# Tile 0's layer norm among tile 1's first products, and low parts issued at once at the joints and in the opening

## The chip, the cores and the metric

The kernel runs on one core of one Trainium2 chip. The metric is the device time of one execution in microseconds. Of the kernel before there are three timed runs, with a median of 1212.61 us (1208.63 to 1213.71), and one profiled execution.

## The reference

A decoder trunk in float32: 256 tokens, model width 1024, two layers. Each layer is a half-step FFN, a mixer and a second half-step FFN, each between two RMS norms (before: `pre`, after: `post`):

```python
for l in range(DEPTH):
    h = rms_norm(x, ffn1_pre_g[l])
    x = x + 0.5 * rms_norm(swiglu(h, ffn1_w1[l], ffn1_w2[l]), ffn1_post_g[l])
    h = rms_norm(x, mix_pre_g[l])
    q, k, v, u_s, v_s, g_a, g_b = jnp.split(h @ w_in[l], IN_SPLIT_POINTS, axis=-1)
    y_attn = sliding_window_attention(q, k, v, attn_sinks[l])
    y_sgu = spatial_gating(gelu(u_s), gelu(v_s), sgu_ln_g[l], sgu_ln_b[l], sgu_w[l], sgu_b[l])
    merged = sigmoid(g_a) * (y_attn @ w_attn_branch[l]) + sigmoid(g_b) * (y_sgu @ w_sgu_branch[l])
    x = x + rms_norm(merged @ w_out[l], mix_post_g[l])
    h = rms_norm(x, ffn2_pre_g[l])
    x = x + 0.5 * rms_norm(swiglu(h, ffn2_w1[l], ffn2_w2[l]), ffn2_post_g[l])
```

FFNs are 2816 wide (SwiGLU). Attention has 16 query heads and 2 key/value heads of 64, a window of 128 and one sink logit for each head. `spatial_gating` takes a layer norm of gelu(v_s) and mixes it over the tokens of a chunk of 128 with a lower triangular matrix. The two branches meet in the merge.

## The kernel before

**Split products.** Every float32 product is done in three passes of TensorE on a reduced format: an operand is split into a high part (its rounding) and a low part (what is left), and high x high, high x low and low x high are summed in a bank (`passes`, L249; `feature_major`, L256 to L258; `feature_pair`, L269). The 256 tokens are two tiles of 128, tile 0 and tile 1.

**Weights.** All weights come as *units*, slices of 128x1024 in the order of use. SP loads a unit into one of four `raw` buffers; ScalarE makes its high part (`wh`, L137), VectorE its low part (`wl`, the subtraction L149). Both go into a ring of nine pairs, or, for the first four units of a sub-layer, into buffers of other tensors (named `m` or `n`). The low part is the last reader of a raw buffer: the load of unit u+4 is issued behind it and waits for it. `Stream.upto(n)` splits all units below n. The low part lags one unit: `upto` issues the cast of unit u, then the low part of unit u-1, and u stays *pending* (`self.rest`) until the next unit is split or a product asks for it:

```python
                self.ready += 1
                self.low()
                self.rest = u
```

**Order.** It is a manual schedule: each engine executes its instructions in the order in which the code emits them. So where a step stands in the code decides what stands behind it in its engine's queue.

**The opening.** The normalisation of the first FFN's input and its first eight units are written out by hand (from L958 on): transposes, the weighing with the gain (`weigh`, L934), splits, products in parts. It ends with `subs[0].prepare()` and `finish`.

**A sub-layer** begins with *first products* (`FirstFFN`: eight units; `FirstMix`: ten, units 0 to 7 for v_s and 8 and 9 for v and k), which have the tokens as rows. `middle` does the rest with features as rows: in an FFN the columns of SwiGLU (first pass L269, sums L624 and L625, Silu L627); in a mixer, pair by pair, u (units 10 to 17), q (units 18 to 25), the gates and the two branches. Attention steps are put into slots of that sequence (`ATTEND`); scores start with L710, which takes q from `evac_q`: ScalarE writes the scaled high part (L834), VectorE the low part (L837).

**A joint** is where one sub-layer's last products and the next one's first meet. There are five: two into mixers, three into FFNs. `project` writes it: a loop over the second matrix's units but the last four; `head(t)`, which finishes tile t's sum with those four (ScalarE squares it, L174; VectorE weighs the result with the post gain, L434); the reciprocal root of the total (`total`, L204; `rsqrt`, L182 to L197); the sum onto x and its weighing with the next gain (L438, L443); transposes (L214, copied by L517, low part L521); the first products of tile 0, of which some steps already run ahead of tile 1's; then tile 1's. Near tile 0's products `st.upto(fence)` splits the next sub-layer's first units, the last of them pending.

In tile 1's loop there is one more step:

```python
            if i == 10:
                turn0()
            s()
            if i % 2:
                st.upto(min(st.ready + 1, first.units[-1] + 1 + AHEAD))
```

`rest` has 12 steps. In a mixer these are four for units 4 to 7 (six products each), then eight for units 8 and 9 (three each); ahead of the loop stand 24 products (`hi + lo`). `turn0` is tile 0's second half of `finish`. In an FFN it transposes the hidden values and splits them. In a mixer it transposes the keys (L375), ScalarE takes their high part (`kth`, L376), VectorE their low part (`ktl`, L379), and then VectorE does tile 0's layer norm of v_s (from L384 on; its last operations are two of 128x1024). Tile 1's (`turn1`) runs during the u products.

Of the kernel before, what the change touches and what calls it, by code (L numbers as in the profile page):

```python
# [63 lines left out]
def trunk(ctx: ExitStack, tc: tile.TileContext, a: dict, out: bass.AP):  # L64
# [24 lines left out]
    def new(p, shape, tag, dt=F32, **kw):  # L89
        ids[0] += 1  # L90
        return p.tile(shape, dt, tag=tag, name=f"{tag}_{ids[0]}", **kw)
# [8 lines left out]
    class Stream:  # L100
        def __init__(self):
            self.src, self.where = [], []
            self.raw, self.split = {}, {}
            self.loaded = self.ready = 0
            self.free = RING
            self.rest = None

        def add(self, src, where="ring"):
            self.src.append(src)
            self.where.append(where)  # L110
            return len(self.src) - 1
# [9 lines left out]
        def upto(self, n, spare=0):  # L121


            while self.ready < min(n, len(self.src)):
                u = self.ready
                if self.where[u] == "ring":
                    if self.free <= spare:
                        return
                    self.free -= 1
                self.load(u + 1)  # L130
                if self.where[u] == "ring":
                    h, lo = new(ring, [P, 1024], "wh", F32R), new(ring, [P, 1024], "wl", F32R)
                else:
                    at = self.where[u]
                    both = new({"m8": m8, "n8": n8}[at], [P, 2, 1024], at, F32R)
                    h, lo = both[:, 0, :], both[:, 1, :]
                nc.scalar.copy(h, self.raw[u])  # L137
                self.split[u] = (h, lo)
                self.ready += 1
                self.low()  # L140
                self.rest = u

        def low(self):

            if self.rest is not None:
                u = self.rest
                self.rest = None
                h, lo = self.split[u]
                nc.vector.tensor_tensor(out=lo, in0=self.raw.pop(u), in1=f(h), op=ALU.subtract)  # L149
                self.load(u + 1 + RAW)  # L150
# [11 lines left out]
    st = Stream()  # L162
# [6 lines left out]
    def halves():  # L169
        return [slice(h * 512, (h + 1) * 512) for h in range(2)]  # L170
# [61 lines left out]
    def spread(dg):  # L232

        n = dg.shape[1]
        ps = bank()[:, 0:n * P]
        nc.tensor.matmul(ps, ones, flat(dg), start=True, stop=True)
        rb = new(t2, [P, n, P], "t2")
        nc.scalar.copy(flat(rb), ps)
        return rb

    def bc4(ap):
        return ap.unsqueeze(1).to_broadcast([P, 4, P])
# [30 lines left out]
    class FirstFFN:  # L273
# [23 lines left out]
            return hi, lo, rest, one  # L297

        late = 11

        def finish(self, t, r, hts):

            o = self.o[t]
            s = new(t2, [P, 512], "t2")
            hh = new(t2, [P, 512], "t2")
            if r is None:
                nc.scalar.activation(s, o[0], AF.Silu)
                nc.vector.tensor_tensor(out=hh, in0=s, in1=o[1], op=ALU.mult)
            else:
                nc.scalar.activation(s, o[0], AF.Silu, scale=r)  # L310
                nc.vector.scalar_tensor_tensor(out=hh, in0=o[1], scalar=r, in1=s, op0=ALU.mult, op1=ALU.mult)

            def turn():
                split(hts[0][0][:, 0:FA, rows_of(t)], hts[0][1][:, 0:FA, rows_of(t)], transpose4(hh, 0))
            return turn

    class FirstMix:
# [33 lines left out]
            return hi, lo, rest  # L351

        late = 6

        def finish(self, t, r, kv):
            vs, vv, kth, ktl, lng, lnb = kv
# [41 lines left out]
    def project(units, lhs, k_post, gpost, gpre, nxt, xt, behind=None):  # L398
# [7 lines left out]
        def one(t, c, h, b):  # L406
            lh, ll = lhs(c)
            wh, wl = st[units[c]]
            passes(o[t][h], lh[:, rows_of(t)], ll[:, rows_of(t)], wh[:, b], wl[:, b], (0, 1, 2), c == 0, c == n - 1)
# [4 lines left out]
        for c in range(n0):  # L414
            if behind:
                behind(c, 0)
            for t in range(NT):
                for h, b in enumerate(halves()):
                    one(t, c, h, b)
            st.done(units[c])  # L420
            if behind:
                behind(c, 1)
            left = n0 - 1 - c
            st.upto(min(end + lead[left], fence) if left < len(lead) else min(units[c] + AHEAD + 1, end))

        parts = [new(tiny2, [P, 2], "parts") for _ in range(NT)]
        og = [new(t4, [P, D], "t4") for _ in range(NT)]
# [17 lines left out]
        def scale(t, r):  # L445
            for b in halves():
                nc.vector.tensor_scalar(out=og[t][:, b], in0=og[t][:, b], scalar1=r, scalar2=None, op0=ALU.mult)
# [60 lines left out]
        first = nxt.first  # L508

        def turn(t, h):  # L510
            return transpose4(og[t], h * 4)

        def quarter(t, h):
            return og[t].rearrange("p (a b) -> p a b", a=KD)[:, h * 4:h * 4 + 4, :]

        def high(t, h, ps):
            nc.scalar.copy(xth[:, h * 4:h * 4 + 4, rows_of(t)], ps)  # L517

        def low(t, h, ps):
            at = (slice(None), slice(h * 4, h * 4 + 4), rows_of(t))  # L520
            nc.vector.tensor_tensor(out=xtl[at], in0=ps, in1=f(xth[at]), op=ALU.subtract)  # L521
# [40 lines left out]
        dg = diagonal([r0])  # L562
        scale(1, rn)
        st.upto(fence)
        for i, s in enumerate(rest):
            if i == first.late:
                turned = [turn(1, h) for h in range(2)]
                for h in range(2):
                    high(1, h, turned[h])
                    low(1, h, turned[h])  # L570
                rb = spread(dg)
                for h in range(2):
                    nc.vector.tensor_tensor(out=quarter(0, h), in0=ps[h], in1=bc4(rb[:, 0, :]), op=ALU.mult)
            s()
        nxt.prepare()
        turn0 = first.finish(0, r0, nxt.into)
# [5 lines left out]
        for i, s in enumerate(rest):  # L582
            if i == 0:
                for h in range(2):
                    high(0, h, quarter(0, h))
                    low(0, h, quarter(0, h))
            if i == 10:
                turn0()
            s()
            if i % 2:  # L590
                st.upto(min(st.ready + 1, first.units[-1] + 1 + AHEAD))
        return first.finish(1, None, nxt.into)

    class FFN:
# [16 lines left out]
        def middle(self, xt, xth, xtl, turn1, early):  # L611
            for _ in range(2):
                self.into.append((new(m8, [P, 8, S], "m8", F32R), new(m8, [P, 8, S], "m8", F32R)))
            for c in range(FA, FC):
                o = [bank(), bank()]
                us = self.cols[(c - FA) * 2:(c - FA) * 2 + 2]
                for half in range(2):
                    feature_pair(o[half], us[half], xt)
                if c == FA + 2:
                    turn1()  # L620
                s = new(t2, [P, 512], "t2")
                y = s.rearrange("p (a b) -> p a b", a=2)
                for half in range(2):
                    nc.scalar.copy(y[:, half, :], o[half][:, S:2 * S])  # L624
                    nc.vector.tensor_tensor(out=y[:, half, :], in0=o[half][:, 0:S], in1=y[:, half, :], op=ALU.add)  # L625
                    if half == 0:
                        nc.scalar.activation(y[:, 0, :], y[:, 0, :], AF.Silu)  # L627
                nc.vector.tensor_tensor(out=y[:, 1, :], in0=y[:, 0, :], in1=y[:, 1, :], op=ALU.mult)
                st.upto(us[1] + 1 + AHEAD)
                hh, hl = self.lhs(c)  # L630
                split(hh, hl, s[:, S:2 * S])
                if c == FA + 2:
                    early()
# [291 lines left out]
    first = subs[0].first  # L925
# [95 lines left out]
    subs[0].prepare()  # L1021
    turns = [first.finish(t, r01[t], subs[0].into) for t in range(NT)]

    def turn1():
        for turn in turns:
            turn()

    for i, sub in enumerate(subs):
        last = i == len(subs) - 1
        nxt = None if last else subs[i + 1]  # L1030
        gains = []

        def early():

            gains.append(gain(sub.post, i // 3))
            if not last:
                gains.append(gain(nxt.pre, (i + 1) // 3))
            if i == 0:
                nc.sync.dma_start(sinks, a["attn_sinks"].unsqueeze(0).partition_broadcast(P))
            if isinstance(nxt, Mix):  # L1040
                nxt.tables()

        behind = sub.middle(both, *xt, turn1, early)
        turn1 = project(sub.rows, sub.lhs, sub.k_post, gains[0], None if last else gains[1], nxt, xt, behind)
# [54 lines left out]
```

## Time and profile before

| | |
|---|---|
| time, median of 3 runs | 1212.61 us (1208.63 to 1213.71) |
| the profiled execution | 1208.95 us, its span 1207.0 us |
| mean granted TensorE clock | 0.993 |
| TensorE matmul busy (PE) | 1179.5 us, 98% |
| TensorE weight load busy (PEld, beside PE) | 1048.6 us, 87% |
| VectorE busy (DVE) | 836.0 us, 69% |
| ScalarE busy (ACT) | 678.4 us, 56% |
| GpSimd busy (POOL) | 60.0 us, 5% |
| moved by DMA | 220.89 MB, mean 183 GB/s |

The span runs from the first to the last recorded instruction; the time of the execution is 1.95 us longer. Busy shares are means over stages that differ: VectorE, at 69%, is full in a joint and has room in between. Of VectorE's 836.0 us, 454.6 are the 372 low parts of weights (L149, 1250 ns each), and of ScalarE's 678.4 the 372 casts take 382.9 (1049 ns each).

### The profile page before, as it was taken

Reading aid. Unit: us, or ns where it says so; the run is one execution under the profiler, and the core shown is the slowest. Engines: PE = TensorE matmul, PEld = TensorE weight load, DVE = VectorE, ACT = ScalarE, POOL = GpSimd, SP = SyncE. Lnnn points to the kernel's source line nnn. Section 1 sums busy time; section 2 is a strip of 40 time slices with the busy share of each in tenths; the row PEclk is TensorE's granted clock in tenths of the full one; section 3 lists DMA queues with packets and bytes.
Section 4 is the critical chain, followed back from the end, with each engine's and each line's share of the span. In section 5 each row is a group of like instructions: output and inputs, shape, how many; then the busy total and the mean of one; then the engine's idle time right before and its main releaser. Section 6 shows DMA issues by size and latency. Waiting matters only on the chain.

```text
span 1207.0 us, 18394 instructions
## 1 busy us (share of the span) xinstructions
PE 1179.5 (98%) x7031; PEld 1048.6 (87%) x7031; DVE 836.0 (69%) x1423; ACT 678.4 (56%) x1143; POOL 60.0 (5%) x40
## 2 busy tenths in 40 slices
PE   8999999999999999999999999999899999999997
PEld 6788888899999888888888888879899997888886
DVE  6768747678775877676576766576868768676653
ACT  5656634457676555655445655454567664665541
POOL 0000000000212200000000000000012030000000
PEclk9999999999999999999999999999999999999999
DMA  6577673465446636658636657735544664555660
GB/s 227 190 244 228 232 237 115 138 241 157 123 145 201 196 105 228 208 178 261 206 102 221 218 181 257 228 102 175 181 152 122 187 194 128 177 206 184 198 211 35
DMA packets 61287, 220.89 MB, mean 183 GB/s; under 512 B 7056, under 2 KB 7056, under 8 KB 61200
## 3 DMA queue, kind: packets, MB, share of 16 engines
q1 hardware_dynamic: 60912, 219.46, 56.0%
q8 instruction: 55, 0.90, 0.3%
q10 hardware_dynamic: 288, 0.27, 0.1%
q14 instruction: 32, 0.26, 0.1%
HBM read 218.65 MB, written 1.05 MB: 182 GB/s over the span
## 4 chain that ended last, share of the span: by engine, by line
PE 83%; DVE 10%; DMA 3%; ACT 2%; issue 1%; SPq 0%; DVEq 0%; ACTq 0%
PE mm L269 32%; PE mm L249 31%; PE mm L256 5%; PE mm L257 5%; PE mm L258 5%; DMA raw<-in_w_in 2%; DVE wl L149 2%; DMA raw<-in_ffn_w 1%; PE mm L747 1%; DVE x L438 1%; DVE rt L193 1%; PE mm L214 1%; ACT wh L137 1%; DVE t L443 1%; PE mm L710 1%
## 5 line engine op out<-in xcount | busy, mean ns | idle before, releaser
L149 DVE TENSOR_TENSOR wl<-raw,wh 128x1024 fp32r<-128x1024 f32 x372 | 454.6, 1250 | 112.8 <-ACT wh L137 111.8
L137 ACT CAST wh<-raw 128x1024 fp32r<-128x1024 f32 x372 | 382.9, 1049 | 183.0 <-DMA raw<-in_ffn_w 76.6
L269 PE MATMUL mm<-xt,wh 128*128 128x512 f32 x1152 | 290.7, 393 | 1.1 <-ACT t L310 0.9
L249 PE MATMUL mm<-wh,m 128*128 128x512 f32 x832 | 258.8, 390 | 0.0
L269 PEld LDWEIGHTS mm<-xt,wh 128*128 128x128 f32 x1152 | 207.6, 189 | 38.5 <-ACT t L310 1.2
L249 PEld LDWEIGHTS mm<-wh,m 128*128 128x128 f32 x832 | 156.3, 188 | 32.1
L269 PEld LDWEIGHTS mm<-xt,wl 128*128 128x128 f32 x1152 | 157.1, 191 | 11.8 <-DVE wl L149 0.6
L249 PE MATMUL mm<-wl,m 128*128 128x512 f32 x416 | 162.1, 390 | 0.0
L269 PE MATMUL mm<-xt,wl 128*128 128x256 f32 x1152 | 160.8, 283 | 0.2 <-DVE wl L149 0.2
L256 PE MATMUL mm<-xt,wh 128*128 128x256 f32 x512 | 147.7, 288 | 0.0
L258 PE MATMUL mm<-xt,wl 128*128 128x256 f32 x512 | 146.2, 286 | 0.0
L257 PE MATMUL mm<-xt,wh 128*128 128x256 f32 x512 | 146.2, 286 | 0.0
L625 DVE TENSOR_TENSOR t<-mm,t 128x256 f32<-128x256 f32 x144 | 60.7, 422 | 97.4 <-ACT t L624 97.4
L256 PEld LDWEIGHTS mm<-xt,wh 128*128 128x128 f32 x512 | 99.7, 195 | 0.2
L257 PEld LDWEIGHTS mm<-xt,wh 128*128 128x128 f32 x512 | 99.6, 195 | 0.2
L258 PEld LDWEIGHTS mm<-xt,wl 128*128 128x128 f32 x512 | 99.5, 194 | 0.0
L249 PEld LDWEIGHTS mm<-wl,m 128*128 128x128 f32 x416 | 78.2, 188 | 15.8
L624 ACT COPY t<-mm 128x256 f32<-128x256 f32 x144 | 52.9, 368 | 46.6 <-PE mm L269 46.3
L256 PE MATMUL mm<-m,wh 128*128 128x256 f32 x256 | 72.7, 284 | 0.0
L258 PE MATMUL mm<-m,wl 128*128 128x256 f32 x256 | 72.5, 283 | 0.0
L257 PE MATMUL mm<-m,wh 128*128 128x256 f32 x256 | 72.5, 283 | 0.0
L627 ACT ACTIVATE t<-t 128x256 f32<-128x256 f32 x72 | 30.1, 418 | 74.8 <-DVE t L625 74.8
(156 smaller groups left out, 1331.4 us busy)
## 6 DMA issues: line engine op xcount, KB each, us to landing
raw<-in_ffn_w SPq DMA_DIRECT2D x264, 512.0 KB, 4.4
raw<-in_w_in SPq DMA_DIRECT2D x84, 512.0 KB, 4.3
raw<-in_w_sgu_branch SPq DMA_DIRECT2D x16, 512.0 KB, 3.6
raw<-in_w_attn_branch SPq DMA_DIRECT2D x16, 512.0 KB, 4.3
raw<-in_w_out SPq DMA_DIRECT2D x16, 512.0 KB, 4.6
gain<-in_ffn_post_g SPq DMA_DIRECT2D x4, 512.0 KB, 5.8
gain<-in_ffn_pre_g SPq DMA_DIRECT2D x3, 512.0 KB, 7.5
x<-in_x SPq DMA_DIRECT2D x4, 256.0 KB, 4.4
```

The lines of the kernel that those rows point to most:

```text
L137: nc.scalar.copy(h, self.raw[u])
L149: nc.vector.tensor_tensor(out=lo, in0=self.raw.pop(u), in1=f(h), op=ALU.subtract)
L193: nc.vector.scalar_tensor_tensor(out=t, in0=y, scalar=w, in1=y, op0=ALU.mult, op1=ALU.mult)
L214: nc.tensor.transpose(ps[:, k, :], src[:, (c0 + k) * P:(c0 + k + 1) * P], ident)
L249: nc.tensor.matmul(o, every[i][0], every[i][1], start=start and i == 0, stop=stop and i == 2)
L256: nc.tensor.matmul(o, wh[:, ks], ah[:, k, :], start=(k == 0), stop=False)
L257: nc.tensor.matmul(o, wh[:, ks], al[:, k, :], start=False, stop=False)
L258: nc.tensor.matmul(o, wl[:, ks], ah[:, k, :], start=False, stop=(k == KD - 1))
L269: nc.tensor.matmul(out_, w[:, k * P:(k + 1) * P], x, start=(i == 0), stop=(i == len(todo) - 1))
L624: nc.scalar.copy(y[:, half, :], o[half][:, S:2 * S])
L625: nc.vector.tensor_tensor(out=y[:, half, :], in0=o[half][:, 0:S], in1=y[:, half, :], op=ALU.add)
L627: nc.scalar.activation(y[:, 0, :], y[:, 0, :], AF.Silu)
```

## The change

Three things are edited.

1. A flag `slip` in `Stream`. While it is false, `upto` issues the low part of a unit right behind its own cast, so that none is pending. It is false in the opening and becomes true behind the first FFN's `finish`.
2. In `project`, `st.low()` behind the loop and again behind `st.upto(fence)`: the pending unit's low part is issued at once. The first place is ahead of `head(0)` and so of L434; the second is ahead of tile 0's remaining first products.
3. `turn0` goes into tile 1's loop at a step that the first products name: 10 for an FFN, as before, and 2 for a mixer.

```diff
@@ class Stream
             self.rest = None
+            self.slip = False
...
                 self.ready += 1
                 self.low()
                 self.rest = u
+                if not self.slip:
+                    self.low()
@@ class FirstFFN
         late = 11
+        turn0 = 10
@@ class FirstMix
         late = 6
+        turn0 = 2
@@ project
             left = n0 - 1 - c
             st.upto(min(end + lead[left], fence) if left < len(lead) else min(units[c] + AHEAD + 1, end))
+        st.low()
...
         scale(1, rn)
         st.upto(fence)
+        st.low()
         for i, s in enumerate(rest):
...
-            if i == 10:
+            if i == first.turn0:
                 turn0()
@@ opening
     turns = [first.finish(t, r01[t], subs[0].into) for t in range(NT)]
 
+    st.slip = True
+
```

In the rows of the programs' order below, a row is line, operation, result<-operands and shape; names carry a serial number, and line numbers of the changed kernel are a few higher. In VectorE's queue at layer 0's joint into the mixer, `wl_1817` is the low part of unit 7, `wl_1823` that of unit 8, `t_347` (before) and `t_348` (now) the weighed sum. Before:

```order
L149 TENSOR_TENSOR wl_1793<-raw_1767,wh_1792 128x1024
L149 TENSOR_TENSOR wl_1799<-raw_1772,wh_1798 128x1024
L149 TENSOR_TENSOR wl_1817<-raw_1778,wh_1816 128x1024
L434 TENSOR_TENSOR t_347_1830<-mm_1468,gain_633 128x512
L204 SCALAR_TENSOR_TENSOR rv_1861<-parts_1828 128x1
```

And now:

```order
L152 TENSOR_TENSOR wl_1793<-raw_1767,wh_1792 128x1024
L152 TENSOR_TENSOR wl_1799<-raw_1772,wh_1798 128x1024
L152 TENSOR_TENSOR wl_1817<-raw_1778,wh_1816 128x1024
L152 TENSOR_TENSOR wl_1823<-raw_1796,wh_1822 128x1024
L440 TENSOR_TENSOR t_348_1833<-mm_1468,gain_633 128x512
```

Unit 8's low part has moved ahead of tile 0's first weighing. Further on in the same queue, in tile 1's first products, `wl_2027` is (before) unit 9's low part, `wl_2161` that of unit 10, the first of u, and the three behind it those of units 11 to 13; `ktl` are the keys' low parts, and BN_STATS begins tile 0's layer norm. Before:

```order
L149 TENSOR_TENSOR wl_2027<-raw_1802,wh_2026 128x1024
L363 TENSOR_SCALAR t_414_2111<-mm_2056,ry_2018 128x2x64 x2
L369 SCALAR_TENSOR_TENSOR vv_2105<-mm_2056,ry_2018,vv_2105 128x2x64
L521 TENSOR_TENSOR xt_349<-t_347_1830,xt_349 128x4x128 x2
L149 TENSOR_TENSOR wl_2161<-raw_1820,wh_2160 128x1024
L149 TENSOR_TENSOR wl_2176<-raw_1826,wh_2175 128x1024
L149 TENSOR_TENSOR wl_2189<-raw_2030,wh_2188 128x1024
L149 TENSOR_TENSOR wl_2201<-raw_2090,wh_2200 128x1024
L379 TENSOR_TENSOR ktl_12_131<-mm_2218,kth_2106 64x2x128
L379 TENSOR_TENSOR ktl_13_132<-mm_2218,kth_2106 64x2x128
L384 BN_STATS st_2224<-n_409_2104 128x6 x2
```

And now (the rows left out are the small operations of the layer norm):

```order
L374 SCALAR_TENSOR_TENSOR vv_2105<-mm_2059,ry_2021,vv_2105 128x2x64
L527 TENSOR_TENSOR xt_352<-t_348_1833,xt_352 128x4x128 x2
L384 TENSOR_TENSOR ktl_12_131<-mm_2163,kth_2106 64x2x128
L384 TENSOR_TENSOR ktl_13_132<-mm_2163,kth_2106 64x2x128
L389 BN_STATS st_2169<-n_409_2104 128x6 x2
...
L398 SCALAR_TENSOR_TENSOR n_409_2104<-n_409_2104,ry_2190,gain_2109 128x1024
L152 TENSOR_TENSOR wl_2161<-raw_1820,wh_2160 128x1024
L152 TENSOR_TENSOR wl_2207<-raw_1826,wh_2206 128x1024
L152 TENSOR_TENSOR wl_2220<-raw_1829,wh_2219 128x1024
L152 TENSOR_TENSOR wl_2232<-raw_2033,wh_2231 128x1024
```

The keys' low parts and the whole layer norm now stand ahead of the low parts of units 10 to 13, and unit 9's is no longer in this stretch but earlier. On TensorE, the keys' transposes stood nearly at the end of tile 1's first products, behind those of unit 8 and half of unit 9 (`mm_2181`). Before:

```order
L249 MATMUL mm_2181<-wh_2026,xt_349 128x256
L249 MATMUL mm_2181<-wl_2027,xt_349 128x256
L249 MATMUL mm_2181<-wh_2026,xt_349 128x256 x2
L249 MATMUL mm_2181<-wl_2027,xt_349 128x256
L249 MATMUL mm_2181<-wh_2026,xt_349 128x256
L375 MATMUL mm_2218<-ident_99,t_414_2111 128x128 x2
L249 MATMUL mm_2181<-wh_2026,xt_349 128x256
```

Now they stand between units 5 and 6 (`wh_1792` and `wh_1798`):

```order
L252 MATMUL mm_2119<-wl_1793,xt_352 128x512
L252 MATMUL mm_2118<-wh_1792,xt_352 128x512
L252 MATMUL mm_2119<-wh_1792,xt_352 128x512
L380 MATMUL mm_2163<-ident_99,t_414_2111 128x128 x2
L252 MATMUL mm_2118<-wh_1798,xt_352 128x512
L252 MATMUL mm_2119<-wh_1798,xt_352 128x512
```

They follow 36 products of tile 1 in place of 66.

## Rows read from the trace of the kernel before

**Rows 1.** TensorE's waits, whole span: engine, line, waited for: us in total, times, longest.

```profile
PE mm L710 <- DVE m L837: 7.5, 3, 5.0
PE mm L249 <- DVE wl L149: 6.8, 5, 2.8
```

**Rows 2.** Timeline, opening: start, duration, engine, line, operation [idle before <-what ended it].

```profile
12.18 0.69 DVE L934 TENSOR_TENSOR t<-mm,g 128x512 f32<-128x512 f32 x1
12.78 1.22 DVE L149 TENSOR_TENSOR m<-raw,m 128x1024 fp32r<-128x1024 f32 x1
...
14.05 8.01 PE L249 MATMUL mm<-m,n 128*128 128x512 f32 x34 [0.87 <-DVE m L149]
...
46.70 0.50 PE L269 MATMUL mm<-xt,wh 128*128 128x512 f32 x1 [0.88 <-ACT t L310]
```

**Rows 3.** Timeline, layer 0's joint into the mixer.

```profile
190.74 1.05 ACT L137 CAST wh<-raw 128x1024 fp32r<-128x1024 f32 x1 [1.05 <-DMA raw<-in_w_in]
...
192.41 0.69 DVE L434 TENSOR_TENSOR t<-mm,gain 128x512 f32<-128x512 f32 x1 [1.46 <-ACT t L174]
...
195.58 0.69 DVE L443 TENSOR_TENSOR t<-x,gain 128x512 f32<-128x512 f32 x1
...
196.42 0.63 PE L214 MATMUL mm<-ident,t 128*128 128x128 f32 x4
...
213.59 1.22 DVE L149 TENSOR_TENSOR wl<-raw,wh 128x1024 fp32r<-128x1024 f32 x1
...
214.86 0.39 PE L249 MATMUL mm<-wl,xt 128*128 128x256 f32 x1 [2.84 <-DVE wl L149]
```

**Rows 4.** Timeline, layer 0's second FFN into layer 1's first.

```profile
596.58 1.05 ACT L137 CAST wh<-raw 128x1024 fp32r<-128x1024 f32 x1 [1.63 <-DMA raw<-in_ffn_w]
...
598.25 0.69 DVE L434 TENSOR_TENSOR t<-mm,gain 128x512 f32<-128x512 f32 x1 [2.04 <-ACT t L174]
...
599.86 0.16 DVE L204 SCALAR_TENSOR_TENSOR rv<-parts 128x1 f32<-128x1 f32 x1 [0.92 <-ACT t L174]
...
616.03 0.50 PE L249 MATMUL mm<-wl,xt 128*128 128x512 f32 x1 [0.39 <-DVE wl L149]
```

**Rows 5.** Timelines of TensorE and VectorE, mixer's first products of tile 1 (809.77: layer 1).

```profile
216.27 7.26 PE L249 MATMUL mm<-m,xt 128*128 128x512 f32 x24
223.37 0.62 PE L249 MATMUL mm<-wh,xt 128*128 128x512 f32 x2
...
230.97 0.38 PE L375 MATMUL mm<-ident,t 128*128 128x128 f32 x2
...
231.86 0.86 DVE L379 TENSOR_TENSOR ktl<-mm,kth 64x256 fp32r<-64x256 f32 x2 [4.62 <-ACT kth L376]
...
232.13 0.28 PE L258 MATMUL mm<-xt,wl 128*128 128x256 f32 x1
...
238.48 1.22 DVE L149 TENSOR_TENSOR wl<-raw,wh 128x1024 fp32r<-128x1024 f32 x1
...
809.77 5.63 PE L249 MATMUL mm<-m,xt 128*128 128x512 f32 x24
```

**Rows 6.** Windows: stretch, us, PE, PEld, DVE, ACT, POOL busy, PEclk, DMA share, GB/s.

```profile
217.00:219.00 2.00, 2.00 (x6) 1.61 (x5) 1.35 (x4) 1.82 (x4) 0.00 (x0) 0.50 1.03 403
282.00:285.00 3.00, 3.00 (x17) 3.00 (x16) 2.97 (x17) 0.00 (x0) 0.00 (x0) 0.55 0.76 212
873.80:876.00 2.20, 2.03 (x9) 1.87 (x9) 2.15 (x3) 2.16 (x3) 0.00 (x0) 0.50 0.74 222
```

**Rows 7.** Timelines around L710 in both layers, and the weight loads, 200 to 285.

```profile
255.84 4.62 DVE L149 TENSOR_TENSOR wl<-raw,wh 128x1024 fp32r<-128x1024 f32 x4
...
279.09 0.33 PE L710 MATMUL mm<-kth,m 128*128 128x128 f32 x1 [2.11 <-DVE m L837]
...
873.85 0.48 PE L710 MATMUL mm<-kth,m 128*128 128x128 f32 x1 [5.00 <-DVE m L837]
...
DMA to landing us min/median/max: 3.6/3.9/7.3
```

## The prediction

> **What bounds the kernel now.** I read the page's busy table first: TensorE works through almost the whole span, so time can come only out of its waits, out of stretches at half clock, or out of the two ends. The list of waits comes second. Under PE the reader is to see two large entries: low parts of the attention queries (L837) ahead of L710, 7.5 us in three waits, and low parts of weights (L149) ahead of L249, 6.8 us in five [rows 1]. Third comes the timeline around each wait, last the granted clock in windows.
>
> The five waits of the second entry are the joints. In layer 0's joint into the mixer, TensorE stands still for 2.84 us ahead of the products of unit 9, whose low part VectorE starts at 213.59, though its copy is much older [rows 3]. The joints into an FFN have 0.39 each, three times [rows 4]. That leaves 6.8 - 2.84 - 1.17 = 2.8 for layer 1's joint into its mixer. The two longest waits for L837 are 2.11 in layer 0 and 5.00 in layer 1 [rows 7].
>
> **The change part by part.** No instruction and no transfer is added or lost; they change places on VectorE, ScalarE and TensorE, and SP's loads, which wait for low parts, go when those do.
>
> Opening. TensorE's wait of 0.87 that ends at 14.05 is for a low part that ran from 12.78, behind the weighing at 12.18 [rows 2]. In the new order it stands ahead of that weighing, so it is over about when TensorE gets there: -0.87. The wait of 0.88 at 46.70 is for ScalarE's L310, which is queued behind casts that wait for loads [rows 2]; each load goes when a low part four units earlier is done, and those now come a unit sooner: up to -0.88. Bounds 0 and -1.75. Between the two lies a chain of ScalarE and VectorE that no longer wait lets go faster, so I take -1.3.
>
> Joints into an FFN. The last unit's low part goes ahead of L434. Its cast ends at 596.58 + 1.05 = 597.63, so it runs to 598.86, and L434 begins there instead of at 598.25. That is hidden: L204, next in line, waits for ScalarE's sum until 599.86 in any case [rows 4]. The wait of 0.39 goes, three times: -1.2. If the cast were 0.4 later, L204 would be late and up to the same amount lost: bounds -1.2 and +0.4.
>
> Joints into a mixer, two. Unit 8's low part likewise goes ahead of L434. Its cast ends at 191.79; it holds VectorE until 193.05; L434 stood at 192.41: 0.64 late. Here nothing hides it: L443 ends at 195.58 + 0.69 = 196.27 and TensorE's transposes of it start at 196.42 [rows 3]. So +0.64 there; then unit 9's low part is made in time and 2.84 go: TensorE comes to tile 1's first products 2.20 earlier, at 216.27 - 2.20 = 214.07.
>
> Layer norm of tile 0. Its transposes (L375) now stand after 36 products of tile 1 instead of near the end. The first 24 took 7.10 us here (to 223.37), against 7.26 - 5.63 = 1.63 less in layer 1 [rows 5]; the reason is the clock, 0.50 at 217 to 219, after the long wait [rows 6]. Without the wait I take 5.47, so 0.228 for each, and 12 more: L375 at 214.07 + 5.47 + 2.74 = 222.3. L379 follows L375 by 0.89, and unit 10's low part follows L379 by 238.48 - 231.86 = 6.62 [rows 5]: it starts at 229.8 and, at 4.62 / 4 = 1.16 each [rows 7], is done at 231.0. It used to be done long before the layer norm; now it is behind it. TensorE needs it after the rest of tile 1. From 223.37 to 232.13 it had 8.76 us of work; 2.74 of it comes before L375 now, so it is there at 222.3 + 6.0 = 228.3 [rows 5]. **A new wait of 2.7 us takes the old one's place**, and what is queued behind it on TensorE are all the u products. Then TensorE goes on at 231.0 instead of 232.13, 1.1 earlier; in layer 1, which has no 1.63 to win back, 0.5 later. At the joint itself the change is worth nearly nothing.
>
> What pays is behind it. VectorE ran the layer norm of tile 0 from 231.86 on, then unit 14's low part, others, and tile 1's layer norm from 255.84 - 6.62 = 249.22, 17.4 after the first [rows 5, 7]. In the new order the first one starts 222.3 + 0.89 = 223.2. Behind it now come the low parts of units 10 to 13 too, and with them loads 14 to 17. Load 14 is issued 7.8 after the first L379, at the median of 3.9 from issue to landing [rows 7] it is there at 11.7; a cast of 1.05 and a low part of 1.2 (and 0.2 between) let load 18 go at 14.2. ScalarE in turn holds the cast of unit 15, tile 1's Gelu and three more casts, so unit 16's low part, and with it load 20, comes at 18.1. Landing at 22.0, cast, ktl: the second layer norm starts 23.5 after the first, at 246.7, **2.5 earlier** than before. The units' order behind it is unchanged, so L837 and L710 follow: 279.09 - 2.5 = 276.6. TensorE gets there at 279.09 - 2.11 - 1.1 = 275.9, so the wait shrinks to 0.7 and layer 0 is 2.5 ahead. Layer 1 by the same steps: TensorE arrives 0.5 later, L837 comes some 2.4 earlier, the wait of 5.00 becomes 2.1, and 2.4 are won. Both: -4.9. Bounds: with landings of 3.6 one more microsecond in all; with the longest, 7.3, two landings in a row cost 6.8, and the layer comes out 4.3 late instead of 2.5 early.
>
> Clock. The stretch 282 to 285, after the wait of 2.11, has 0.55, so 1.35 us lost; 873.8 to 876, after 5.00, has 0.50, so 1.1 lost [rows 6]. With a wait of 0.7 I count the first as won, with 2.1 half of the second: -1.9; bounds 0 and -2.5. The 1.63 at the joint is in the steps above already.
>
> The new waits of 2.7 may bring such stretches too: the ones of 2.84, 2.11 and 5.00 did, layer 1's of 2.8 did not, as 5.63 shows [rows 5, 6]. The Trainium skill's page "TensorE: Matmul & The Clock Gate", in "HAM oscillation - how this bites in real kernels", says that a kernel whose TensorE runs idle between bursts falls to half clock each time and pays for each. By it both new waits would cost 1.6 more ahead of L710: TensorE would arrive in layer 0 at 277.5 instead of 276.6, 0.9 lost, and in layer 1 still ahead of L837; the sum would be 8.4 instead of 9.3. Three of this trace's four long waits bear the rule out; I leave the 0.9 in the range.
>
> Sum: 1.3 + 1.2 + 4.9 + 1.9 = 9.3. The profiled execution took 1208.95 us (span 1207.0 and 1.95 around it), so 1199.7 by it; the median of the three runs is 3.66 higher, at 1212.61. I set 9.3 against the median: **1203.3 us**.
>
> **The rivals.**
>
> The joint's wait is only moved. For: the new wait of 2.7 is as long as the old, and loads 14 to 17, which used to be issued at leisure during tile 1's products, now go in one burst with 18 to 20 close behind. Against: four transfers spaced 1.16 apart landed in 3.9 at the median. If landings take 5.15, the two generations eat the 2.5 and the mixers give nothing, nor the clock: 1.3 + 1.2 = 2.5, so 1210.1.
>
> The burst of loads starves the mixer. The same mechanism beyond that point: each load waits for the ones ahead of it, and with 7.3 a landing, as the longest row has [rows 7], L710 goes 4.3 later than before in each layer: 8.6 - 2.5 = 6.1 slower, 1218.7. It decides from landings of 5.15 on. For it: 7.3 did occur. Against: that one had two gain tables ahead of it in SP's queue, which are not there in this burst.
>
> **How the numbers follow.** Forecast 0.67, moved wait 0.24, starved mixer 0.07, and 0.02 for something better than all of it. The forecast's own range is 1199 (all bounds won) to 1207 (the opening and the clock give nothing); the range for 8 in 10 takes in the moved wait and reaches from 1198 to 1211. What a measurement here can tell from no change is 0.5%, 6 us: faster below 1206.5. The forecast lies below that but for its upper edge (0.02); with the 0.02 that makes 0.67 faster, 0.26 the same, 0.07 slower.
>
> **What would show it.** Right: no TensorE wait for L149 in joints into an FFN; transposes in the mixer's joint about 0.6 later against the products ahead of them; a wait of about 2.7 on unit 10's low part at the first u product of both layers; unit 20's low part some 2.5 earlier against the joint; waits at L710 below 1 and about 2. Wrong: if L710 still waits 2 and 5, or loads 14 to 20 land in over 5 us, the gain is only that of the opening and the FFN joints; if the opening's wait for L310 is still there, 0.9 is missing.

## The result and the profile after

The changed kernel takes 1202.11 us (median of 10 runs, 1196.81 to 1207.33) against 1210.9 (10 runs); the ratio is 0.9921, 95% interval 0.9902 to 0.9941: 9.6 us faster, 7.1 to 11.9 (8.8 by the medians). The forecast was 9.3, at 1203.3. Its profiled execution took 1199.29. The time came out as forecast, but not for the reason given: the early layer norm, which was to bring more than half of it, brings nothing that these runs can tell, and the low parts bring it all.

TensorE's waits after (engine, line, waited for: us in total, times, longest) show what went and what came:

```profile
PE mm L261 <- DVE wl L152: 5.0, 2, 2.5
PE mm L717 <- DVE m L844: 4.1, 4, 1.8
PE mm L970 <- POOL ident masks.py:199: 1.4, 1, 1.4
PE mm L252 <- ACT m L138: 1.4, 2, 0.8
PE mm L217 <- DVE t L449: 0.9, 2, 0.5
PE mm L272 <- DVE xt L948: 0.7, 1, 0.7
```

The 6.8 us of L249 for low parts [rows 1] are gone. The first row is the new wait at the first u product, in each layer. L717 (L710 before) keeps 4.1 of 7.5. The last row stands in the opening and was 0.2 before. The fifth row is the price at a mixer's joint, seen in the timeline of that joint in layer 0:

```profile
189.38 1.23 DVE L152 TENSOR_TENSOR wl<-raw,wh 128x1024 fp32r<-128x1024 f32 x1 [1.15 <-ACT wh L138]
...
190.52 0.69 DVE L440 TENSOR_TENSOR t<-mm,gain 128x512 f32<-128x512 f32 x1
...
193.69 0.69 DVE L449 TENSOR_TENSOR t<-x,gain 128x512 f32<-128x512 f32 x1
...
194.53 0.63 PE L217 MATMUL mm<-ident,t 128*128 128x128 f32 x4 [0.51 <-DVE t L449]
```

Unit 8's low part runs directly ahead of L440, and everything behind it slides: TensorE, which had no such wait ahead of the transposes [rows 3], now waits 0.51.

The timelines of layer 0 behind that joint answer to [rows 5, 7]:

```profile
220.38 0.86 DVE L384 TENSOR_TENSOR ktl<-mm,kth 64x256 fp32r<-64x256 f32 x2 [5.79 <-ACT kth L381]
...
227.01 4.63 DVE L152 TENSOR_TENSOR wl<-raw,wh 128x1024 fp32r<-128x1024 f32 x4
...
228.28 0.58 PE L261 MATMUL mm<-xt,wl 128*128 128x256 f32 x1 [2.55 <-DVE wl L152]
...
245.04 1.05 ACT L138 CAST wh<-raw 128x1024 fp32r<-128x1024 f32 x1 [1.93 <-DMA raw<-in_w_in]
245.99 0.36 ACT L381 CAST kth<-mm 128x256 fp32r<-128x256 f32 x1
...
246.39 0.86 DVE L384 TENSOR_TENSOR ktl<-mm,kth 64x256 fp32r<-64x256 f32 x2 [2.02 <-ACT kth L381]
...
276.48 0.33 PE L717 MATMUL mm<-kth,m 128*128 128x128 f32 x1 [1.83 <-DVE m L844]
...
866.66 0.33 PE L717 MATMUL mm<-kth,m 128*128 128x128 f32 x1 [1.50 <-DVE m L844]
```

Tile 0's layer norm begins at 220.38; behind it, at 227.01, come the low parts of units 10 to 13, and TensorE waits 2.55 for the first. Tile 1's layer norm begins at 246.39, held up by a cast that waited for its load. The last row is the first scores of layer 1. The windows of TensorE's clock:

```profile
228.30:231.30 3.00, 3.00 (x14) 3.00 (x15) 3.00 (x3) 0.00 (x0) 0.00 (x0) 0.50 0.66 172
276.60:280.00 3.40, 3.03 (x25) 2.91 (x26) 3.37 (x4) 2.52 (x3) 0.00 (x0) 1.00 0.46 157
818.90:821.90 3.00, 3.00 (x14) 3.00 (x15) 3.00 (x3) 0.00 (x0) 0.00 (x0) 0.50 0.66 195
866.80:870.00 3.20, 2.82 (x23) 2.71 (x24) 3.17 (x4) 2.51 (x3) 0.00 (x0) 1.00 0.58 172
```

Behind both waits at u the granted clock is 0.50 (1.2 GHz), behind both waits at L717 it is 1.00; before, the half clock stood behind L710 [rows 6].

A ledger of the change is had by subtracting the start of the same TensorE product in the two traces, place by place (196.42 [rows 3] against 194.53 is -1.89, for instance). The difference between two places is what the stretch between them gained:

| stretch | forecast | traces |
|---|---|---|
| opening | -1.3 | -2.41 |
| layer 0: joint, up to the transposes | +0.64 | +0.52 |
| unit 9's wait, and its half clock | -4.47 | -4.66 |
| new wait at u | +2.7 | +2.64 |
| half clock behind it | 0 | +1.52 |
| from there to the first scores | -1.4 | -0.28 |
| half clock behind the scores | -1.35 | -1.46 |
| **layer 0's mixer** | **-3.9** | **-1.7** |
| layer 1: joint | +0.64 | +0.44 |
| unit 9's wait | -2.84 | -2.96 |
| new wait at u, and its half clock | +2.7 | +2.55 + 1.52 |
| from there to the first scores | -2.9 | -3.51 |
| half clock behind the scores | -0.55 | -1.70 |
| **layer 1's mixer** | **-2.95** | **-3.65** |
| three joints into an FFN | -1.2 | -1.7 |
| **sum** | **-9.3** | **-9.4** |

The rows on the clock hold for one execution of each kernel. The ten executions of the changed kernel reach from 1196.81 us, at a mean granted clock of 0.997, to 1207.33 us, at 0.989: how much half clock comes is not the same in each.

### The profile page after: what moved, and what is told of

Same layout as the page of the kernel before. It is cut to its first block, busy times and chain, and to the rows that moved or that the text cites. A ratio compares the mean times of both kernels' runs of the same rounds, so it can differ in the third digit from the quotient of the medians.

```text
span 1197.6 us, 18409 instructions
## 1 busy us (share of the span) xinstructions
PE 1176.7 (98%) x7031; PEld 1047.8 (87%) x7031; DVE 835.8 (70%) x1423; ACT 677.9 (57%) x1143; POOL 60.0 (5%) x40
## 4 chain that ended last, share of the span: by engine, by line
PE 87%; DVE 6%; DMA 3%; ACT 1%; issue 1%; SPq 0%; DVEq 0%; ACTq 0%
PE mm L272 34%; PE mm L252 31%; PE mm L261 6%; PE mm L259 6%; PE mm L260 6%; DMA raw<-in_w_in 3%; DVE wl L152 2%; PE mm L217 1%; PE mm L754 1%; ACT wh L138 1%; DMA raw<-in_ffn_w 1%; PE mm L717 1%; PE mm L718 1%; PE mm L767 0%; PE mm L766 0%
## 5 line engine op out<-in xcount | busy, mean ns | idle before, releaser
L152 DVE TENSOR_TENSOR wl<-raw,wh 128x1024 fp32r<-128x1024 f32 x372 | 454.6, 1251 | 114.2 <-ACT wh L138 113.5
```

## The experiments

Each has its edit, what was expected, and the ratio to the kernel before, run beside it on the same chip, with its 95% interval. Runs of different chips are compared by these ratios; where the medians say something else, they stand beside them. "Layer norm early" is `turn0 = 2` in the mixer. The first four take the change apart.

**open_only.** The flag alone (edit 1); against the changed kernel:

```diff
@@ class FirstMix
-        turn0 = 2
+        turn0 = 10
@@ project, behind the loop and behind st.upto(fence)
-        st.low()
```

> The flag in the opening alone; no low part added in project, turn0 = 10 for both. The two profiles of before and after differ by 2.41 us at the first wait-free L269 products behind the opening. If that is the opening's own worth: 2.4 us faster than before, the waits of 0.87 at 14.05 and 0.88 at 46.70 gone, everything behind it as before (waits of 2.8 at both mixers' joints, 2.1 and 5.0 at L710). If the prediction's bound of 1.75 holds and the rest is one execution against another: 1.3 to 1.75.

0.9984 (0.9974 to 0.9995): 1.9 us faster, 0.6 to 3.1. The waits at the joints and at the scores are still there (6.7 us for L152; 6.9 for L842, in its profile). The opening gives about 1.9; the interval holds both expectations.

**low_only.** Edits 1 and 2 without 3, `turn0 = 10` in both:

> Both low-part edits, layer norm left where it was (turn0 = 10). Theory A, the low parts carry the change: tile 1's products begin 2.45 earlier at both mixers, layer 0's half clock there (1.67) goes, no wait of 2.55 on unit 10's low part appears, the layer norm follows TensorE and comes as much earlier, so the waits for the queries' low parts stay at 2.1 and 5.0 with their half clock (1.46 and 1.70): 2.4 + 1.6 + 4.1 + 2.45 = 10.5 faster than before, no slower than the changed kernel (9.4 in its profile). Theory B, the prediction's: the early layer norm pays; with it at the end, the loads and not TensorE set tile 1's layer norm, the waits for the queries' low parts grow by what the joints gave, and only opening and FFN joints are won: 4.0 faster than before, 5 slower than the changed kernel.

0.9908 (0.9894 to 0.9921): 11.1 faster than before. It is at least as fast as the whole change (0.9902 to 0.9941): theory B is out. VectorE's timeline shows why:

```profile
215.34 3.50 DVE L152 TENSOR_TENSOR wl<-raw,wh 128x1024 fp32r<-128x1024 f32 x3 [0.18 <-ACT wh L138]
219.97 1.23 DVE L152 TENSOR_TENSOR wl<-raw,wh 128x1024 fp32r<-128x1024 f32 x1 [1.14 <-ACT wh L138]
225.81 0.86 DVE L384 TENSOR_TENSOR ktl<-mm,kth 64x256 fp32r<-64x256 f32 x2 [4.62 <-ACT kth L381]
...
243.54 0.86 DVE L384 TENSOR_TENSOR ktl<-mm,kth 64x256 fp32r<-64x256 f32 x2 [1.24 <-ACT kth L381]
...
272.80 1.41 DVE L844 SCALAR_TENSOR_TENSOR m<-mm,m 64x512 fp32r<-64x512 f32 x2
```

Tile 0's layer norm begins at 225.81, 5.4 later than in the changed kernel, and tile 1's at 243.54, 2.9 *earlier*. The low parts of units 10 to 13 run in the gap ahead of it (215.34 to 221.20) and send loads 14 to 17 off, so the second generation is there in time. The first scores, and the clock behind them, in the timeline of TensorE and in the windows:

```profile
273.54 0.33 PE L717 MATMUL mm<-kth,m 128*128 128x128 f32 x1 [2.61 <-DVE m L844]
...
863.71 0.33 PE L717 MATMUL mm<-kth,m 128*128 128x128 f32 x1 [3.06 <-DVE m L844]
```

```profile
228.30:231.30 3.00, 3.00 (x27) 3.00 (x27) 2.72 (x11) 0.00 (x0) 0.00 (x0) 1.00 0.00 0
273.80:280.00 6.20, 5.92 (x28) 5.76 (x28) 6.04 (x23) 2.64 (x4) 0.00 (x0) 0.50 0.72 215
```

No wait at u, full clock there; what is left is the wait at the scores. Set against the changed kernel, TensorE comes to the first scores 2.94 earlier in layer 0 (273.54 for 276.48) and 2.95 earlier in layer 1 (863.71 for 866.66). The half clock behind them, which the changed kernel's profiled execution did not have, gives 2.7 and 2.9 of that back. So the two profiles end level (1199.03 and 1199.29) by what the clock did in one execution of each.

**turn_only.** Edit 3 alone:

> The early layer norm alone (turn0 = 2 in the mixer), no low part moved. Theory A: the joints' waits of 2.97 stay, the new waits of 2.55 and their half clock come on top, and tile 1's layer norm does not come earlier: layer 0 some 1.7 slower, layer 1 some 0.5 faster, in all 0 to 3 slower than before. Theory B: 4 to 5 faster than before, with the waits for the queries' low parts below 1 and about 2.

1.0037 (1.0020 to 1.0054): 4.5 slower, 2.4 to 6.5; theory B expected 4 to 5 faster. The size went beyond theory A's upper end, though the interval reaches into its range. Its waits hold both lists, the old and the new:

```profile
PE mm L252 <- DVE wl L152: 6.8, 5, 2.8
PE mm L261 <- DVE wl L152: 5.0, 2, 2.5
PE mm L715 <- DVE m L842: 3.8, 3, 1.7
```

The waits at its first scores are 1.67 and 1.72, much like the changed kernel's 1.83 and 1.50. But here half clock follows both:

```profile
282.80:286.00 3.20, 3.08 (x13) 2.92 (x14) 3.17 (x4) 2.62 (x3) 0.00 (x0) 0.50 0.59 166
880.50:885.00 4.50, 4.45 (x21) 4.48 (x22) 4.47 (x14) 1.90 (x2) 0.00 (x0) 0.50 0.64 205
```

**low10.** The changed kernel with unit 10's low part ahead of the early layer norm:

```diff
             if i == first.turn0:
+                if first.turn0 < 10:
+                    st.low()
                 turn0()
```

> The changed kernel with one more line: unit 10's low part is issued ahead of turn0 in the mixers, so ahead of the keys' low parts and the layer norm, in VectorE's idle time there (5.8 us ahead of L384). Both theories: no wait at the first u product, no half clock behind it, so TensorE is 2.55 + 1.5 = 4.1 earlier there in both layers. Theory A: what the queries' low parts wait for lies in VectorE's and the loads' own chain, which gets at most 1.1 shorter; the waits at L717 grow from 1.8 to some 4.8, with half clock behind: 0 to 2 faster than the changed kernel. Theory B: the wait at u is what the early layer norm costs; it is won in both layers: 6 to 8 faster than the changed kernel.

0.9914 (0.9900 to 0.9928). The wait at u is gone, and it is within 1 us of the changed kernel's 0.9921, as theory A had it: the 4 us that TensorE wins at u in each layer it gives back at the scores, by longer waits and by half clock behind them (0.50 behind both, 1.00 in the changed kernel):

```profile
PE mm L719 <- DVE m L846: 8.4, 3, 4.9
...
273.72 0.33 PE L719 MATMUL mm<-kth,m 128*128 128x128 f32 x1 [3.08 <-DVE m L846]
...
864.46 0.47 PE L719 MATMUL mm<-kth,m 128*128 128x128 f32 x1 [4.90 <-DVE m L846]
```

The next four ask what the wait at the scores hangs on.

**low_gate.** low_only with two of four gating steps later:

```diff
-GATING = (9, 10, 11, 12)
+GATING = (9, 10, 15, 17)
```

> low_only with the third and fourth gating steps moved from q units 3 and 4 to q unit 7 and the first gb unit but one (GATING = 9, 10, 15, 17). Theory A: L717 waits for VectorE, which in layer 0 of low_only is busy nearly without a break from 263 to 277 and has 4 x 2.07 us of gating additions and products (L691, L694, L698) among the low parts ahead of the second L844; two of the four go behind it, 4.1 us, so L844 is bounded by ScalarE's L841 (done at 269.8, TensorE arrives at 270.4): the waits of 3.1 fall below 1 and the half clock behind them (6.8 us long in both layers, worth up to 3.4 each) goes: 4 to 9 faster than low_only. Rival C: the wait is for the weight loads, VectorE merely spends the same time idle instead: within 1 of low_only.

0.9864 (0.9840 to 0.9888), 5.3 faster than low_only by the ratios, 3.4 by the medians, and the two intervals don't meet: rival C is out, VectorE's queue is what L717 waits for. It was less clean than expected: the waits fell to 1.01 and 1.66, and half clock still follows both, as TensorE's timeline and the windows show:

```profile
272.36 0.33 PE L717 MATMUL mm<-kth,m 128*128 128x128 f32 x1 [1.01 <-DVE m L844]
...
859.64 0.33 PE L717 MATMUL mm<-kth,m 128*128 128x128 f32 x1 [1.66 <-DVE m L844]
```

```profile
274.60:277.50 2.90, 2.90 (x16) 2.90 (x16) 2.87 (x16) 1.96 (x2) 0.00 (x0) 0.50 0.86 250
861.80:864.80 3.00, 3.00 (x16) 3.00 (x16) 2.97 (x16) 1.80 (x2) 0.00 (x0) 0.50 0.79 246
```

**low_att.** low_only with one unit of q ahead of the first scores:

```diff
-ATTEND = (27, 32, 38, 44, 50, 56)
+ATTEND = (29, 32, 38, 44, 50, 56)
```

> low_only with the first attention step one unit later on TensorE (ATTEND 29 instead of 27). One unit of q, 2.9 us of products, goes ahead of L717, so its wait of 3.1 falls below 0.5 with its half clock: 4 to 8 faster than low_only if nothing behind it is late; rival: the scores' reduction and softmax come 2.9 later and a wait of that size shows up at the probabilities' transposes or at the second attention step: within 1 of low_only.

0.9819 (0.9796 to 0.9841): 10.8 faster than low_only by the ratios, 9.3 by the medians, more than expected. Nothing late shows up behind it. Layer 0 has no wait there now and full clock all through its mixer; layer 1, against the expectation, keeps a wait of 2.75 (first row the waits of both layers, second the window of layer 0's mixer):

```profile
PE mm L717 <- DVE m L844: 3.1, 2, 2.8
...
200.00:300.00 100.00, 100.00 (x771) 96.81 (x770) 80.59 (x163) 57.67 (x104) 4.66 (x2) 1.00 0.51 169
```

**before_att.** The same number in the kernel before, nothing else:

> The kernel before, with the first attention step one unit later (ATTEND 29) and nothing of the change. If what bounds a mixer is the wait at its first scores, and not the joint: 2.9 us of q products go ahead of L710, the waits of 2.11 and 5.00 become 0 and 2.1, the half clock behind them (3.4 and 6.8 us long, costing 1.46 and 1.70) goes in part: 6 to 8 faster than before, nearly as much as the whole change (8.8). If TensorE merely waits later for the same thing: within 1.5 of before.

0.9930 (0.9914 to 0.9946): 8.5 faster by the ratio, 7.6 by the medians, for the 6 to 8 expected. One number in a table is worth nearly as much as the whole change (9.6), with the joints' waits untouched:

```profile
PE mm L249 <- DVE wl L149: 6.8, 5, 2.8
...
PE mm L710 <- DVE m L837: 1.6, 4, 0.5
```

**low10_gate.** low10 with low_gate's slots:

> The kernel low10 (layer norm early, unit 10's low part ahead of it) with the same gating slots as low_gate. If an early layer norm is worth anything, it is here, where VectorE's queue ahead of L844 is shorter and the wait at u is gone: then faster than low_gate by 1 to 3; if the layer norm's place is of no account once low parts are on time: within 1 of low_gate, 4 to 9 faster than low10, whose waits there are 8.4 in all.

0.9874 (0.9855 to 0.9894), against low_gate's 0.9864: not the 1 to 3 faster by which an early layer norm would have shown its worth. The intervals overlap; the layer norm's place again makes no difference that these runs can tell.

The last four price the layer norm where the scores no longer hide it, and look for the best.

**after_att.** The changed kernel with `ATTEND` 29; it differs from low_att in the layer norm's place alone:

> The changed kernel with ATTEND 29. From low_att (1188.6, layer norm late) it differs only in the layer norm's place. Theory A: with the wait at L717 gone, nothing takes up the waits of 2.55 on unit 10's low part and their half clock (1.5) any more; they are exposed in layer 0, and in layer 1 offset what is left of the wait at L717 (2.8): 2 to 5 slower than low_att, 1191 to 1193. Theory B: the early layer norm takes the wait in layer 1 away and costs nothing elsewhere: 2 to 4 faster than low_att.

0.9890 (0.9874 to 0.9907) against 0.9819 (0.9796 to 0.9841): some 8.5 slower by the ratios, 6.9 by the medians (1195.48 and 1188.61), more than expected. The waits at L717 are gone from its list and those at u stand alone:

```profile
PE mm L261 <- DVE wl L152: 5.0, 2, 2.5
```

The granted clock is 0.50 behind both. So the early layer norm costs time. How much is less sure: the two profiled executions differ by 5.3 (1195.74 and 1190.42), and 1.5 of that is there ahead of the first mixer, where the two kernels don't differ (half clock in the opening of one of them). In the changed kernel shorter waits at the scores, and full clock behind them, made up for the cost.

**low10_att.** low10 with `ATTEND` 29:

> low10 (layer norm early, unit 10's low part ahead of it, all low-part edits) with ATTEND 29. low_att, which has the layer norm late and is otherwise the same, has 1188.6 and still one wait of 2.8 ahead of L717 in layer 1. Theory A (the layer norm's place is of no account, since VectorE's and the loads' chain sets L844): within 1.5 of low_att, the wait in layer 1 still 2 to 4. Theory B (an early layer norm brings L844 earlier): that wait and its half clock go, 3 to 5 faster than low_att.

0.9843 (0.9823 to 0.9863), with low_att's interval overlapping: 2.9 slower by the ratios, 2.1 by the medians. Theory B, 3 to 5 faster, is out; theory A's "within 1.5" these runs can't tell. Its detail did not come: the wait in layer 1 is below 1, the longest is 1.4 in all. So with unit 10's low part ahead of it the early layer norm does shorten that wait, but half clock follows in both layers, and no time is won.

**low_late8.** low_only, with unit 8's low part ahead of `head(0)` only where an FFN follows:

```diff
-        st.low()
+        if isinstance(nxt, FFN):
+            st.low()
```

> low_only, but ahead of head(0) the pending low part is issued only at joints into an FFN; unit 8's comes behind the cast of unit 9, with unit 9's right behind it. Theory: the 0.44 to 0.52 by which the changed kernel is late at the two mixers' first transposes (L217 <- L449) are the price of unit 8's low part ahead of L440; they come back, unit 9's low part ends some 1.2 later but still 1 ahead of its product: 0.9 to 1.0 faster than low_only. Rival: with two low parts in a row the wait at unit 9 comes back, up to 1.2 at each of the two: 0 to 1.5 slower.

0.9884 (0.9863 to 0.9905) against 0.9908 (0.9894 to 0.9921), 2.9 faster by the ratios and 0.7 by the medians: the intervals overlap, so the time doesn't settle it. No wait for low parts comes back, so the rival is out. In the traces the stretch from the sub-layer's start to the joint's transposes is 0.15 (layer 0) and 0.42 (layer 1) shorter: at most 0.6 in all.

**late8_att_gate.** low_only with `ATTEND` 29, `GATING = (9, 10, 11, 15)` and low_late8's edit:

> low_only with ATTEND 29, the fourth gating step at q unit 7 (GATING = 9, 10, 11, 15) and unit 8's low part only behind unit 9's cast at the mixers' joints. From low_att: the wait of 2.8 in layer 1 loses the 2.07 us of VectorE's work that moves behind L844, and its half clock (1.7); the joints 0 to 0.5 each: 2 to 5 faster than low_att, 1184 to 1187. Rival: the late gating step collides with the first softmax on VectorE and a wait appears behind: within 1 of low_att.

0.9821 (0.9803 to 0.9840), 1187.87: the same as low_att within the intervals, though the waits at the scores are all but gone and the clock is full through both mixers:

```profile
PE mm L718 <- DVE m L845: 0.6, 2, 0.4
```

```profile
200.00:300.00 100.00, 99.83 (x772) 96.73 (x771) 80.65 (x163) 57.26 (x104) 4.66 (x2) 1.00 0.52 174
800.00:900.00 100.00, 99.22 (x805) 97.61 (x804) 77.41 (x156) 59.28 (x117) 8.15 (x3) 1.00 0.52 169
```

So the 2 to 5 that were expected don't show: the medians (1187.87 and 1188.61) are 0.7 apart, less than the spread of either. Both beat the changed kernel, by 12 by the ratios and 14 by the medians.

## Why the prediction was right, and where it was not

**Opening.** Both waits went, as forecast, though one of 0.7 for VectorE's split of the transposed input (xt) came up that had been 0.2. The value of 1.3 lay below the 1.9 (0.6 to 3.1) of open_only. The bound of 1.75 counted only TensorE's idle time; the profile's 2.4 is beyond it, but within open_only's interval.

**Joints into an FFN.** Right in kind: no wait for a low part is left and L434's delay is hidden. The size was 0.4 to 0.6 each for 0.39.

**Joints into a mixer.** +0.64 for unit 8's low part was 0.5 and 0.4; unit 9's wait and layer 0's half clock went as worked out (4.7 for 4.5).

**The new wait.** Forecast at 2.7 on unit 10's low part at the first u product, measured 2.55 and 2.47. Here VectorE's order gave the answer, and the durations from the trace of before the number.

**The clock behind it.** The forecast counted nothing there and left 0.9 in its range. Both waits were followed by half clock, at 1.5 each, as the rule of the Trainium skill's "TensorE: Matmul & The Clock Gate" (section "HAM oscillation - how this bites in real kernels") would have had it (in the kernel that it tells of, TensorE idles between short bursts, falls to half clock each time and pays for it each time); the 1.6 that the forecast had worked out for that case from the joint's rows agrees with the 1.5 of the trace. But the waits of 1.83 and 1.50 at L717 in the same trace were followed by full clock, while 1.67 and 1.72 there in turn_only, and 1.01 and 1.66 in low_gate, were followed by half. Nor was "layer 1's of 2.8 did not" a property of that joint. The same wait of 2.83 at the same place was followed by full clock in the kernel before and by half clock in before_att, which differs only in the attention's slots (the first row is before, the second before_att):

```profile
808.30:811.00 2.70, 2.65 (x17) 2.43 (x18) 0.61 (x2) 0.33 (x2) 0.00 (x0) 1.00 0.58 147
...
807.50:810.50 3.00, 3.00 (x14) 2.83 (x14) 0.60 (x2) 0.00 (x0) 0.00 (x0) 0.51 0.77 240
```

The length of a wait alone doesn't tell it.

**"What pays is behind it."** This is the step that failed, twice over.

Its size first. The second layer norm was to start 23.5 after the first; it started 26.0 (layer 0) and 24.9 (layer 1) after. The chain was right up to the issue of load 20 (forecast 18.1 behind the first L379; unit 16's low part ended 18.4 behind it). The landing was wrong: 3.9 is the median of all loads from 200 to 285 [rows 7], most of them issued far apart, and not, as the prediction says, of four spaced 1.16 apart. The trace of before had loads in closer order: the six that it issued from 230 to 250 landed in 4.6 at the median (the first row below). In the changed kernel the answer for the loads issued from 236 to 243 reads as the second row:

```profile
raw<-in_w_in SPq DMA_DIRECT2D x6, 512.0 KB, 4.6
...
DMA to landing us min/median/max: 4.2/6.2/6.4
```

That is the prediction's own sign of being wrong, landings of over 5.

So layer 0 gained 0.3 ahead of the scores instead of 1.4 (waits of 1.83 and 1.50 remained for 0.7 and 2.1): close to the rival in which the joint's wait is only moved. Layer 0's mixer gave 2.2 less than forecast. That was covered up by the opening (1.1 more), the joints into an FFN (0.5 more) and layer 1's mixer (0.7 more, all of it by the clock behind its scores, 1.70 for 0.55). So that the total came out at 9.6 for 9.3 is in good part luck, the clock above all: behind waits as short, turn_only had half clock at the same place.

Then its comparison. The early layer norm was set against the *old* time of the late one. Once the joint's wait is gone, the late one comes earlier too, with TensorE, and still has the low parts of units 10 to 13 in front of it, which keep the loads going. low_only shows that: its second layer norm is 2.9 ahead of the changed kernel's. What edit 3 is worth had to be asked against edits 1 and 2, not against the kernel before. By low_only against after it is worth nothing that these runs can tell; by turn_only it costs 4.5, by after_att some 4 to 8.

**What was not seen at all.** What bounded these mixers was the wait at the first scores, 7.5 in [rows 1], with its half clock, at least as much as the joint. The prediction treated it as something that a faster joint would run into. One unit of independent q products put ahead of it takes away nearly all of it.

What stays open: why half clock follows a wait of 1.01 and not one of 1.83, or the same wait of 2.83 in one execution and not in another; how much of late8_att_gate's smaller wait is gained; and why the landings in the changed kernel's second group of loads are longer than in its first (median 4.8 for those issued from 226 to 232), though both were issued about 1.1 apart.

## What to carry to other kernels

Where a change has several parts, price each against the kernel that has the others, for a step that is left alone also moves when what is ahead of it does. A step pulled forward on a busy engine pushes back what it overtakes; if that is the reader that frees the load buffers, the price comes a generation of loads later, and in a burst the landing is longer than a median over all loads shows. And before shortening the way to a wait, look whether independent work that is needed anyway can be put in front of it.

## What the runs showed of the hardware that was not expected

The landing of a 512 KB load went from a median of 3.9 us over all loads (200 to 285, before) [rows 7] to 6.2 for four issued about 1.1 apart (236 to 243, after). Half clock cost 1.5 to 1.7 us at each of the places in the ledger, over half of the wait of 2.5 that precedes it at u, and 2.7 and 2.9 behind the scores of low_only, so a wait at TensorE can be dearer than its row in the list says. And a wait of 2.5 at u was each time followed by half clock (after, turn_only, after_att), while shorter ones at the scores were (1.01 and 1.66, low_gate; 1.67 and 1.72, turn_only) and were not (1.83 and 1.50, after), and one of 2.83 at layer 1's joint was not in before and was in before_att.
